# Output projection of a two-layer mixer trunk: 512 columns of w_out at a time instead of 256

## The chip, the cores and the metric

The kernel runs on one core of one Trainium2 chip. The core has five engines that run side by side: PE (TensorE: matmuls, and PEld for its weight loads), DVE (VectorE), ACT (ScalarE), POOL (GpSimd) and SP (SyncE, which here issues the DMAs). The metric is the time of one execution on the device in microseconds (us); the median of several runs counts.

## The reference, cut to what matters

Two layers run over 1024 latent tokens and 256 context tokens of 1024 channels each. At the end of a layer the three branches are merged and go through one output projection, whose result is gated and added to the stream:

```python
def _mixer_out(fa, za, u, vs, zb, attn, zc, g, w_s, b_s, w_pa, w_pb, w_pc, w_out):
    ...
    merged = ga * (ya @ w_pa) + gb * (yb @ w_pb) + gc * (yc @ w_pc)
    return merged @ w_out
...
        if not last:
            ...
            xc = xc + gate_c * out_c
        x = x + gate[:, None, :] * out
```

`w_out` is 1024 x 1024 for each layer. The context tokens are projected in layer 0 only, since nothing reads them after layer 1.

## The kernel before, in words

All of it is float32 work done as float32r: each operand is split into a rounded part and a rest (hi and lo), and `mm3` makes three matmuls of one product, hi·hi, hi·lo and lo·hi. Weights come in granules: `granule` loads 512 KB into a tile `raw` (two buffers), ACT copies it to `whi` (five buffers), DVE subtracts to get `wlo` (five buffers). A granule is thus one DMA, one ACT instruction (L212), one DVE instruction (L213).

The output projection is `out_phase`. Tokens are taken in groups: in layer 0 "C" (256 context tokens, two tiles of 128), "0" and "1" (512 latent tokens each, four tiles); in layer 1 "0" and "1". For each group it goes through `w_out` in four steps `n` of 256 columns. `w_tm` fetches a step as two granules of 512 rows x 256 columns. Within a step each tile of 128 tokens takes 24 matmuls (8 row blocks `k`, three each) into one PSUM bank, with the tokens as the stationary operand (`H[g]`, tiles named hh0C, hl1C, hh, hl, ...) and the weights as the moving one. Banks alternate between the tags `s` (three of them) and `mm` (two). Then DVE multiplies with the gate into `og` (L924) and POOL adds to the stream tile `x` (L926). When a group is done its `x` tiles are stored (L934 and L936), and in layer 0 `modulate` makes the next layer's operands of them: squares on ACT (L271), a power on POOL (L273 and L274), a scaling on DVE (L276), transposes on PE (L280) and the copies of L282 to L284.

During the first step of a group the next group's operands are made (`operands`: a load of `dM` into `ld`, L904 on ACT and L905 on DVE) and its `x` tiles are loaded (`load`, L294). SP issues all DMAs in one queue, in order, and holds at one whose buffer isn't free yet.

The order of instructions on each engine is not that of the code. A scheduler at build time moves them by its own estimates of their durations; the tiles' pools decide what has to wait for what. A pool opened where another was closed takes over its addresses, and a tile in it waits for those that lay there. `out_phase` has its small tiles in the pool `gp` (the gates `gb` 8 KB for each partition, `ld` 4 x 2 KB, `og` 4 x 1 KB). When it closes in layer 0, the next layer's `attention` opens `kp` on the same side (`kk` and `vt`, 10 KB each), and then `np`, whose first tile is `rope` (2 KB), loaded at L417 and read on POOL at L317.

Of the kernel before, what the change touches and what calls it, by code (L numbers as in the profile page):

```python
# [11 lines left out]
F32 = mybir.dt.float32  # L12
# [3 lines left out]
ALU = mybir.AluOpType  # L16
# [7 lines left out]
KC = D // 128  # L24
# [42 lines left out]
def trunk_kernel(ctx: ExitStack, tc: tile.TileContext, a: dict, out: bass.AP):  # L67
    nc = tc.nc
    PE, ACT, DVE, POOL = nc.tensor, nc.scalar, nc.vector, nc.gpsimd
# [15 lines left out]
    def bank(tag):  # L85
        tags = banks["tags"]
        tag = tag if tag in tags else "g"
        return banks["pool"].tile([128, 512], F32, tag, bufs=tags[tag])
# [118 lines left out]
    def granule(src, shape):  # L207
        raw = wp.tile(shape, F32, "raw", bufs=2)
        nc.sync.dma_start(raw, src)
        hi = wp.tile(shape, F32R, "whi", bufs=5)  # L210
        lo = wp.tile(shape, F32R, "wlo", bufs=5)
        ACT.copy(hi, raw)  # L212
        DVE.tensor_tensor(lo, raw, hi.bitcast(F32), ALU.subtract)  # L213
        return hi, lo
# [5 lines left out]
    def w_tm(w, c0):  # L220

        r = []
        for half in range(2):
            src = w[half * 512:(half + 1) * 512, c0:c0 + 256].rearrange("(k p) c -> p k c", p=128)
            r.append(granule(src, [128, 4, 256]))
        return r

    def mm3(o, lh, ll, rh, rl, start, stop):
        PE.matmul(o, lh, rh, start=start, stop=False)  # L229
        PE.matmul(o, lh, rl, start=False, stop=False)  # L230
        PE.matmul(o, ll, rh, start=False, stop=stop)  # L231
# [6 lines left out]
    def proj_tm(o, wt, h, t0):  # L238

        for k in range(KC):  # L240
            wh, wl = wt[k // 4]
            mm3(o[:, 0:256], h[0][k][:, t0:t0 + 128], h[1][k][:, t0:t0 + 128],
                wh[:, k % 4, :], wl[:, k % 4, :], k == 0, k == KC - 1)

    H = {}
# [5 lines left out]
    def new_h(g):  # L251

        n = GROUPS[g][1]
        pool = bigs["C" if g == "C" else "L"]
        halves = [[pool.tile([128, KC // 2, n], F32R, f"h{x}{i}{g}") for i in range(2)] for x in "hl"]
        H[g] = [[halves[x][k // 4][:, k % 4, :] for k in range(KC)] for x in range(2)]
        return H[g]
# [6 lines left out]
    def modulate(l, g, xts, pool):  # L264
        v = 1 if g == "C" else 0
        n = len(xts)
        hh, hl = new_h(g)
        ss = pool.tile([128, 4], F32, "ss", bufs=2)
        for i, xt in enumerate(xts):
            junk = ta().bitcast(BF16)  # L270
            ACT.activation(junk, xt, AF.Square, accum_out=ss[:, i:i + 1])  # L271
        rs = pool.tile([128, 4], F32, "rs", bufs=2)
        POOL.tensor_scalar(rs[:, :n], ss[:, :n], 1.0 / D, EPS, ALU.mult, ALU.add)  # L273
        POOL.tensor_tensor(rs[:, :n], rs[:, :n], mhalf[:, :n], ALU.pow)  # L274
        for i in range(n):
            DVE.tensor_scalar(xts[i], xts[i], rs[:, i:i + 1], None, ALU.mult)  # L276
        for k in range(KC):
            p = bank("pt")
            for i in range(n):
                PE.transpose(p[:, i * 128:(i + 1) * 128], xts[i][:, k * 128:(k + 1) * 128], ident)  # L280
            h32 = ta(n * 128)
            ACT.activation(h32, p[:, :n * 128], AF.Identity, scale=adac[l][:, 8 + k, v:v + 1], bias=adac[l][:, k, v:v + 1])  # L282
            POOL.tensor_scalar(hh[k], h32, 1.0, 0.0, ALU.mult, ALU.add)
            DVE.tensor_tensor(hl[k], h32, hh[k].bitcast(F32), ALU.subtract)  # L284

    def load_x(xp, l, t):
        xt = xp.tile([128, D], F32, "x", bufs=8)
        if t >= SEQ:
            src = a["ctx"][0, t - SEQ:t - SEQ + 128, :]
        elif l == 0:  # L290
            src = a["x"][0, t:t + 128, :]
        else:
            src = x1[t // 128]
        nc.sync.dma_start(xt, src)  # L294
        return xt
# [115 lines left out]
    def attention(l, groups, sideA, sideB, xp, wkv, X, S):  # L411
# [35 lines left out]
        def prepare(u):  # L447
            kv, g, t, pr = units[u]
            if (kv, t) not in Q:
                if kv not in W:  # L450
                    W[kv] = w_tm(a["w_in"][l], C_Q + kv * 256)
                Q[kv, t] = queries(W[kv], g, t)

        wt = wkv or w_tm(a["w_in"][l], C_KV)
        ib = 0
        names = ("C", "0", "1")
# [86 lines left out]
    def fetched(st, src, n=512, bufs=4, tag="ld"):  # L543
        t = st.tile([128, 512], F32, tag, bufs=bufs)[:, :n]
        nc.sync.dma_start(t, src)
        return t
# [7 lines left out]
    def rows(l, groups, name, col, S, st):  # L554
        w = w_tm(a["w_in"][l], col)
        for g in groups:
            g0, n = GROUPS[g]
            for i in range(n // 128):
                p = bank("mm")
                proj_tm(p, w, H[g], i * 128)  # L560
                s = staged(st, 256)
                ACT.copy(s, p[:, 0:256])
                nc.sync.dma_start(stored(S, (name, g0 // 128 + i), 256), s)
                yield 256
# [322 lines left out]
    def out_phase(l, groups, xp, gp, last, S):  # L887

        gb = gp.tile([128, 2, D], F32, "gb")
        nv = 1 if last else 2  # L890
        for v in range(nv):
            row = dp.tile([KC, 128], F32, f"gate{l}{v}")
            nc.sync.dma_start(row.rearrange("j p -> p j"), adac[l][:, 16:24, v])
            nc.sync.dma_start(gb[:, v, :], row.rearrange("j p -> (j p)").partition_broadcast(128))
        X, wt = {}, {}
        order = [g for gs in groups for g in gs]

        def operands(g):
            if g == "C":
                return  # L900
            hh, hl = new_h(g)
            for k in range(KC):
                m = fetched(gp, S["M", k, g])
                ACT.activation(hh[k], m, AF.Copy, scale=0.5)  # L904
                DVE.scalar_tensor_tensor(hl[k], m, 0.5, hh[k].bitcast(F32), ALU.mult, ALU.subtract)  # L905

        def load(g):
            g0, n = GROUPS[g]
            X[g] = [load_x(xp, l, g0 + i * 128) for i in range(n // 128)]

        wt[0] = w_tm(a["w_out"][l], 0)
        if order[0] != "C":
            operands(order[0])
        load(order[0])
        for ig, g in enumerate(order):
            gs = [g]
            for n in range(4):
                w = wt.pop(n) if n in wt else w_tm(a["w_out"][l], n * 256)
                v = 1 if g == "C" else 0
                for i, xt in enumerate(X[g]):  # L920
                    p = bank("mm" if i % 2 else "s")
                    proj_tm(p, w, H[g], i * 128)
                    t = gp.tile([128, 256], F32, "og", bufs=4)
                    DVE.tensor_tensor(t, p[:, 0:256], gb[:, v, n * 256:(n + 1) * 256], ALU.mult)  # L924
                    xs = xt[:, n * 256:(n + 1) * 256]
                    POOL.tensor_tensor(xs, xs, t, ALU.add)  # L926
                if n == 0 and ig + 1 < len(order):
                    operands(order[ig + 1])
                    load(order[ig + 1])
            for g in gs:  # L930
                g0, _ = GROUPS[g]
                for i, xt in enumerate(X[g]):
                    if last:
                        nc.sync.dma_start(out[0, g0 + i * 128:g0 + (i + 1) * 128, :], xt)  # L934
                    elif g != "C":
                        nc.sync.dma_start(x1[g0 // 128 + i], xt)  # L936
            if not last:
                for g in gs:
                    modulate(l + 1, g, X[g], xp)
# [25 lines left out]
    for l in range(DEPTH):  # L965
# [58 lines left out]
        for g in groups:  # L1024
            g0, n = GROUPS[g]
# [23 lines left out]
        xp = Pool(tc, name="xp", bufs=1, side=A)  # L1049
        gp = Pool(tc, name="gp", bufs=1, side=B)  # L1050
        out_phase(l, [["0"], ["1"]] if last else [["C"], ["0"], ["1"]], xp, gp, last, S)
        gp.close()
    xp.close()
# [62 lines left out]
```

## Time and profile before

| | |
|---|---|
| runs | 1968.52, 1967.72 and 2089.09 us, median 1968.52 |
| the profiled execution's own time | 1967.06 us |
| span of its profile | 1965.3 us |
| output projection, layer 0, group C | 985.04 to 1010.93 us of the span |
| output projection, layer 0, groups 0 and 1 | 1010.93 to 1108.40 us |
| output projection, layer 1 | 1868.09 to 1960.40 us |

The span runs from the first to the last instruction that the profiler recorded; the execution's own time has some 2 us more around it. A time such as 1010.93 is one on the span's own clock. A matmul's record starts when it is issued, and its end is modelled, so consecutive records overlap: what a matmul takes in a stream is read from the distance between two starts.

### The profile page before, as it was taken

The page shows a single profiled execution, that of the slowest core. Times are in us where ns is not written, and L with a number is a line of the kernel's source. Part 1 is how long each engine was busy: PE and PEld are TensorE (multiplying, and loading weights), DVE is VectorE, ACT ScalarE, POOL GpSimd, SP SyncE. Part 2 cuts the span into 40 slices and gives each one's busy share as a digit, 9 for nine tenths or more (in the row PEclk, how much of TensorE's full clock was granted, in tenths as well). Part 3 has the DMA queues.
Part 4 walks back from the last instruction along what each step waited for, and adds up shares of the span by engine and source line. Part 5 has one row for each costly group of instructions (what it writes and reads, how often), then busy time and mean ns, then how long its engine had stood idle before and what let it go on. Part 6 is the DMA issues. An engine that isn't in the chain of part 4 may idle for free.

```text
span 1965.3 us, 32941 instructions
## 1 busy us (share of the span) xinstructions
PE 1901.6 (97%) x11887; PEld 1688.0 (86%) x11887; DVE 1087.8 (55%) x2211; ACT 799.5 (41%) x2090; POOL 627.5 (32%) x1011
## 2 busy tenths in 40 slices
PE   7989999999999999999999989999999999999999
PEld 2888999999988887888899989899888888888898
DVE  4664665556655648766355455676665655622342
ACT  2653565445644422111243435565554443111320
POOL 1563344533331112211235543344432021211132
PEclk9999999999999999999999999999999999999999
DMA  8431121212565677654464312122134568632462
GB/s 309 119 99 64 50 68 54 79 44 84 163 188 164 188 226 227 171 174 141 148 229 165 108 47 75 54 61 82 34 91 149 158 186 270 191 106 82 134 225 87
DMA packets 281147, 259.91 MB, mean 132 GB/s; under 512 B 20824, under 2 KB 234520, under 8 KB 280984
## 3 DMA queue, kind: packets, MB, share of 16 engines
q1 hardware_dynamic: 280984, 257.80, 41.7%
q8 instruction: 94, 1.54, 0.3%
q14 instruction: 69, 0.57, 0.1%
HBM read 196.91 MB, written 60.83 MB: 131 GB/s over the span
## 4 chain that ended last, share of the span: by engine, by line
PE 82%; DMA 6%; DVE 5%; ACT 3%; issue 2%; POOL 2%; SPq 1%; POOLq 0%; DVEq 0%; ACTq 0%
PE mm L229 16%; PE mm L230 16%; PE mm L231 16%; PE s L230 6%; PE s L229 6%; PE s L231 6%; PE pt L391 3%; PE o L399 2%; PE o L398 2%; PE s L363 1%; PE s L356 1%; DVE wlo L213 1%; DMA raw<-in_w_in_dram 1%; PE s L166 1%; PE s L357 1%
## 5 line engine op out<-in xcount | busy, mean ns | idle before, releaser
L212 ACT CAST whi<-raw 128x1024 fp32r<-128x1024 f32 (+2 forms) x210 | 202.2, 966 | 393.7 <-PE s L230 144.6
L213 DVE TENSOR_TENSOR wlo<-raw,whi 128x1024 fp32r<-128x1024 f32 (+2 forms) x210 | 243.9, 1164 | 213.7 <-ACT whi L212 209.4
L229 PE MATMUL mm<-hh,whi 128*128 128x512 f32 (+1 forms) x768 | 296.2, 386 | 6.6 <-DVE st L552 4.2
L231 PE MATMUL mm<-hh,wlo 128*128 128x512 f32 (+1 forms) x768 | 294.2, 383 | 0.7 <-DVE wlo L213 0.7
L230 PE MATMUL mm<-hl,whi 128*128 128x512 f32 (+1 forms) x768 | 294.4, 383 | 0.0
L229 PE MATMUL mm<-whi,hh 128*128 128x256 f32 x832 | 239.7, 288 | 6.6 <-DVE qt L439 2.5
L231 PE MATMUL mm<-whi,hl 128*128 128x256 f32 x832 | 237.5, 285 | 0.0
L230 PE MATMUL mm<-wlo,hh 128*128 128x256 f32 x832 | 237.3, 285 | 0.0
L674 POOL TENSOR_TENSOR m<-m,tb 128x512 f32<-128x512 f32 x64 | 87.2, 1364 | 409.5 <-DVE tb L673 366.8
L229 PEld LDWEIGHTS mm<-hh,whi 128*128 128x128 f32 x768 | 145.2, 189 | 33.6 <-DVE st L552 5.1
L231 PEld LDWEIGHTS mm<-hh,wlo 128*128 128x128 f32 x768 | 145.1, 189 | 27.7 <-DVE wlo L213 0.9
L229 PEld LDWEIGHTS mm<-whi,hh 128*128 128x128 f32 x832 | 160.3, 193 | 9.0 <-issue 3.1
L230 PEld LDWEIGHTS mm<-hl,whi 128*128 128x128 f32 x768 | 145.3, 189 | 25.3
L231 PEld LDWEIGHTS mm<-whi,hl 128*128 128x128 f32 x832 | 160.5, 193 | 0.2 <-DVE hl L284 0.2
L230 PEld LDWEIGHTS mm<-wlo,hh 128*128 128x128 f32 x832 | 160.4, 193 | 0.2
L379 POOL TENSOR_SCALAR P<-P,rd 128x640 f32<-128x640 f32 (+2 forms) x144 | 110.7, 780 | 105.7 <-DVE rd L377 64.1
L230 PE MATMUL s<-hl,whi 128*128 128x512 f32 x352 | 137.5, 391 | 0.0
L229 PE MATMUL s<-hh,whi 128*128 128x512 f32 x352 | 137.4, 390 | 0.0
L231 PE MATMUL s<-hh,wlo 128*128 128x512 f32 x352 | 137.2, 390 | 0.0
L261 DVE TENSOR_TENSOR pl<-pt,ph 128x512 fp32r<-128x512 f32 (+1 forms) x184 | 112.4, 616 | 39.5 <-ACT ph L260 36.3
L260 ACT CAST ph<-pt 128x512 fp32r<-128x512 f32 (+1 forms) x184 | 96.1, 535 | 32.6 <-PE o L398 18.7
L196 DVE SCALAR_TENSOR_TENSOR aacc<-araw,scol,aacc 128x256 f32<-128x256 f32 x196 | 102.9, 558 | 5.2 <-DMA araw<-in_w_ada_dram 2.8
(303 smaller groups left out, 4637.1 us busy)
## 6 DMA issues: line engine op xcount, KB each, us to landing
raw<-in_w_in_dram SPq DMA_DIRECT2D x122, 512.0 KB, 4.1
araw<-in_w_ada_dram SPq DMA_DIRECT2D x48, 512.0 KB, 6.0
raw<-in_w_out_dram SPq DMA_DIRECT2D x40, 512.0 KB, 3.9
dP<-st SPq DMA_DIRECT2D x64, 256.0 KB, 2.7
lp<-dP SPq DMA_DIRECT2D x64, 256.0 KB, 4.2
x<-in_x_dram SPq DMA_DIRECT2D x16, 512.0 KB, 9.3
raw<-in_w_pc_dram SPq DMA_DIRECT2D x32, 256.0 KB, 2.9
dM<-m SPq DMA_DIRECT2D x32, 256.0 KB, 3.6
```

The lines of the kernel that those rows point to most:

```text
L196: DVE.scalar_tensor_tensor(acc[:, v, :], raws[k // 4][:, k % 4, :], sc, acc[:, v, :], ALU.mult, ALU.add)
L212: ACT.copy(hi, raw)
L213: DVE.tensor_tensor(lo, raw, hi.bitcast(F32), ALU.subtract)
L229: PE.matmul(o, lh, rh, start=start, stop=False)
L230: PE.matmul(o, lh, rl, start=False, stop=False)
L231: PE.matmul(o, ll, rh, start=False, stop=stop)
L260: ACT.copy(hi, src)
L261: DVE.tensor_tensor(lo, src, hi.bitcast(F32), ALU.subtract)
L379: POOL.tensor_scalar(P[hh][:, :nl + 256], P[hh][:, :nl + 256], rd[:, hh:hh + 1], 1.0, ALU.mult, ALU.mult)
L391: PE.transpose(b[:, (2 * i + hh) * 128:(2 * i + hh + 1) * 128], P[hh][:, (i0 + i) * 128:(i0 + i + 1) * 128], ident)
L398: PE.matmul(po, vs, ph[:, i * 256:(i + 1) * 256], start=(i0 + i == 0), stop=False)
L674: POOL.tensor_tensor(m, m, s, ALU.add)
```

## The change

`w_out` is now taken in two steps of 512 columns. A new function fetches a step as four granules of 256 rows x 512 columns (still 512 KB each, so 40 granules over both layers as before), every matmul of the projection has 512 moving columns in place of 256, DVE and POOL handle 512 columns at a time, and `og` has three buffers of 2 KB in place of four of 1 KB.

```diff
+    def w_half(w, n):
+
+        r = []
+        for q in range(4):
+            src = w[q * 256:(q + 1) * 256, n * 512:(n + 1) * 512].rearrange("(k p) c -> p k c", p=128)
+            r.append(granule(src, [128, 2, 512]))
+        return r
...
-        wt[0] = w_tm(a["w_out"][l], 0)
+        wt[0] = w_half(a["w_out"][l], 0)
...
-            for n in range(4):
-                w = wt.pop(n) if n in wt else w_tm(a["w_out"][l], n * 256)
+            for n in range(2):
+                w = wt.pop(n) if n in wt else w_half(a["w_out"][l], n)
                 v = 1 if g == "C" else 0
                 for i, xt in enumerate(X[g]):
                     p = bank("mm" if i % 2 else "s")
-                    proj_tm(p, w, H[g], i * 128)
-                    t = gp.tile([128, 256], F32, "og", bufs=4)
-                    DVE.tensor_tensor(t, p[:, 0:256], gb[:, v, n * 256:(n + 1) * 256], ALU.mult)
-                    xs = xt[:, n * 256:(n + 1) * 256]
+                    for k in range(KC):
+                        wh, wl = w[k // 2]
+                        c = slice(i * 128, (i + 1) * 128)
+                        mm3(p, H[g][0][k][:, c], H[g][1][k][:, c], wh[:, k % 2, :], wl[:, k % 2, :], k == 0, k == KC - 1)
+                    t = gp.tile([128, 512], F32, "og", bufs=3)
+                    DVE.tensor_tensor(t, p, gb[:, v, n * 512:(n + 1) * 512], ALU.mult)
+                    xs = xt[:, n * 512:(n + 1) * 512]
                     POOL.tensor_tensor(xs, xs, t, ALU.add)
```

The new function shifts the lines behind it by eight, so that L229 to L231 of `mm3` are L237 to L239 in the changed kernel, and so on; the text uses the numbers of the kernel before. The scheduler's order is the same up to the first output projection, and again from some way into layer 1's attention to the second one, on every engine. Three places where it differs follow.

PE, layer 1, group 0, from one step of `n` to the next. Before (the last two rows of one tile, then the next step's first tile, whose granule holds four row blocks):

```order
L230 MATMUL mm_21409<-wlo_21278,hh10_21282 128x256
L231 MATMUL mm_21409<-whi_21277,hl10_21284 128x256
L229 MATMUL s_21493<-whi_21483,hh00_21281 128x256
L230 MATMUL s_21493<-wlo_21484,hh00_21281 128x256
L231 MATMUL s_21493<-whi_21483,hl00_21283 128x256
```

And the same place with the change, from the end of the first tile's work on the second half's first granule (whi_20935 and wlo_20936 are its two parts, whi_20941 the rounded part of the second granule):

```order
L238 MATMUL s_20957<-wlo_20936,hh00_20733 128x512
L239 MATMUL s_20957<-whi_20935,hl00_20735 128x512
L237 MATMUL s_20957<-whi_20941,hh00_20733 128x512
L237 MATMUL mm_20985<-whi_20935,hh00_20733 128x512
L238 MATMUL mm_20985<-wlo_20936,hh00_20733 128x512
L239 MATMUL mm_20985<-whi_20935,hl00_20735 128x512
```

Before, a tile's 24 matmuls stand together; now the first two tiles of the second half are interleaved, granule by granule, so that the fourth granule is first needed 29 matmuls into the half and not 18.

SP, layer 0, in the middle of group C (dM_7_1 is the last stored piece of group 1's operands, `x` of in_ctx and in_x the stream tiles, raw the granules of w_out). Before:

```order
L728 DMA dM_7_1_11344<-m1_11099 128x512
L294 DMA x_11374<-in_ctx_dram 128x1024
L294 DMA x_11376<-in_ctx_dram 128x1024
L294 DMA x_11470<-in_x_dram 128x1024
L294 DMA x_11472<-in_x_dram 128x1024
L294 DMA x_11474<-in_x_dram 128x1024
L294 DMA x_11476<-in_x_dram 128x1024
L209 DMA raw_11620<-in_w_out_dram 128x4x256
L209 DMA raw_11752<-in_w_out_dram 128x4x256
L545 DMA ld_11908<-dM_7_1_11344 128x512
L294 DMA x_11912<-in_x_dram 128x1024
L294 DMA x_11914<-in_x_dram 128x1024
```

With the change (the first raw here is the last granule of group C, the second the first of group 0):

```order
L736 DMA dM_7_1_11344<-m1_11099 128x512
L302 DMA x_11386<-in_ctx_dram 128x1024
L302 DMA x_11388<-in_ctx_dram 128x1024
L302 DMA x_11482<-in_x_dram 128x1024
L302 DMA x_11484<-in_x_dram 128x1024
L302 DMA x_11486<-in_x_dram 128x1024
L302 DMA x_11488<-in_x_dram 128x1024
L553 DMA ld_11808<-dM_7_1_11344 128x512
L209 DMA raw_11508<-in_w_out_dram 128x2x512
L302 DMA x_11812<-in_x_dram 128x1024
L209 DMA raw_11640<-in_w_out_dram 128x2x512
L302 DMA x_11814<-in_x_dram 128x1024
```

Both have the same loads behind the store; the granule that group C ends on now stands behind the `ld` load as well, and the first granule of group 0 behind one more `x`.

POOL, from the last stream additions of layer 0 into layer 1 (rs and s are the norms' powers, cg the rotary tables times the gains, qf the keys of group C). Before:

```order
L926 TENSOR_TENSOR x<-x,og 128x256 x10
L273 TENSOR_SCALAR rs<-ss 128x4
L274 TENSOR_TENSOR rs<-rs,mhalf 128x4
L304 TENSOR_SCALAR s_13034<-s_13034 128x2
L305 TENSOR_TENSOR s_13034<-s_13034,mhalf 128x2
L304 TENSOR_SCALAR s_13071<-s_13071 128x2
L305 TENSOR_TENSOR s_13071<-s_13071,mhalf 128x2
L313 TENSOR_TENSOR qf<-tb,gain 128x128 x2
```

With the change:

```order
L937 TENSOR_TENSOR x<-x,og 128x512 x4
L281 TENSOR_SCALAR rs<-ss 128x4
L282 TENSOR_TENSOR rs<-rs,mhalf 128x4
L312 TENSOR_SCALAR s_12474<-s_12474 128x2
L313 TENSOR_TENSOR s_12474<-s_12474,mhalf 128x2
L312 TENSOR_SCALAR s_12511<-s_12511 128x2
L313 TENSOR_TENSOR s_12511<-s_12511,mhalf 128x2
L325 TENSOR_TENSOR cg<-rope,gain 128x64 x4
L321 TENSOR_TENSOR qf<-tb,gain 128x128 x2
```

The first four instructions on the table `rope`, which stood among the gates of layer 0 before, now stand here; and the load of `rope` on SP, which stood between the `ld` loads ahead of group C, now stands right behind the store of group 1's last `x` tile.

## Rows read from the trace of the kernel before

**Rows 1.** The page, part 1: busy time of each engine.

```profile
PE 1901.6 (97%) x11887; PEld 1688.0 (86%) x11887; DVE 1087.8 (55%) x2211; ACT 799.5 (41%) x2090; POOL 627.5 (32%) x1011
```

**Rows 2.** Windows of the output projection: length, busy times (counts), granted clock, DMA share, GB/s.

```profile
985.04:1010.93 25.89, 23.54 (x193) 23.13 (x192) 12.96 (x19) 8.24 (x11) 5.94 (x8) 1.00 0.86 294
1010.93:1108.40 97.47, 97.47 (x820) 97.47 (x819) 49.78 (x72) 38.75 (x53) 45.78 (x53) 1.00 0.45 150
1868.09:1960.40 92.31, 92.31 (x769) 92.10 (x767) 32.69 (x50) 15.56 (x17) 30.07 (x32) 1.00 0.44 155
```

**Rows 3.** Timeline of PE: start, duration, engine, line, operation.

```profile
964.63 0.40 PE L229 MATMUL mm<-hh,whi 128*128 128x512 f32 x1
...
985.04 0.28 PE L229 MATMUL s<-whi,hh0C 128*128 128x256 f32 x1
...
1002.31 0.28 PE L229 MATMUL s<-whi,hh0C 128*128 128x256 f32 x1
```

**Rows 4.** Timeline of SP in group C of layer 0: the issues.

```profile
989.59 0.32 SPq L728 DMA_DIRECT2D dM<-m  x1
...
990.91 2.60 SPq L294 DMA_DIRECT2D x<-in_x_dram  x4
993.61 1.21 SPq L209 DMA_DIRECT2D raw<-in_w_out_dram  x2
996.36 1.33 SPq L545 DMA_DIRECT2D ld<-dM  x1
```

**Rows 5.** The chain that ended last, in group C: start, length, what.

```profile
993.61 12.15 DMA raw<-in_w_out_dram
1005.84 1.05 ACT whi L212
1006.92 1.24 DVE wlo L213
1008.20 0.38 PE s L230
```

**Rows 6.** DMA issues, windows 1011 to 1108 and 1868 to 1960: KB each, median us to landing.

```profile
raw<-in_w_out_dram SPq DMA_DIRECT2D x13, 512.0 KB, 4.6
...
raw<-in_w_out_dram SPq DMA_DIRECT2D x10, 512.0 KB, 3.4
```

**Rows 7.** Timeline of ACT in layer 1's projection: in brackets the idle time before.

```profile
1889.89 1.05 ACT L212 CAST whi<-raw 128x1024 fp32r<-128x1024 f32 x1 [6.37 <-PE mm L231]
```

**Rows 8.** Timeline of DVE, POOL and SP: evictions, a 512-wide one of each, the end.

```profile
1870.33 0.68 DVE L673 SCALAR_TENSOR_TENSOR tb<-ta,pt 128x512 f32<-128x512 f32 x1
1960.51 0.42 DVE L924 TENSOR_TENSOR og<-mm,gb 128x256 f32<-128x256 f32 x1 [2.45 <-PE mm L231]
988.27 1.30 POOL L674 TENSOR_TENSOR m<-m,tb 128x512 f32<-128x512 f32 x1 [4.41 <-DVE tb L673]
1961.02 0.72 POOL L926 TENSOR_TENSOR x<-x,og 128x256 f32<-128x256 f32 x1 [2.14 <-DVE og L924]
```

**Rows 9.** Timeline of POOL, SP, DVE and PE from layer 0 into layer 1.

```profile
971.94 2.52 POOL L317 TENSOR_TENSOR cg<-rope,gain 128x64 f32<-128x64 f32 x4
...
1101.16 8.96 SPq L936 DMA_DIRECT2D x<-x  x4
...
1113.18 2.74 DVE L276 TENSOR_SCALAR x<-x,rs 128x1024 f32<-128x1024 f32 x4 [1.19 <-POOL rs L274]
...
1116.72 0.89 POOL L313 TENSOR_TENSOR qf<-tb,gain 128x128 f32<-128x128 f32 x2
...
1119.32 1.82 POOL L283 TENSOR_SCALAR hh<-ta 128x512 fp32r<-128x512 f32 x2
...
1118.14 0.38 PE L280 MATMUL pt<-ident,x 128*128 128x128 f32 x2
```

**Rows 10.** Windows right behind it, columns as in rows 2.

```profile
1131.00:1141.00 10.00, 10.00 (x86) 9.98 (x84) 7.21 (x23) 2.52 (x13) 6.74 (x17) 1.00 0.00 0
1141.00:1151.00 10.00, 6.12 (x34) 5.32 (x32) 4.85 (x10) 3.45 (x18) 5.48 (x10) 0.83 0.01 2
```

## The prediction

> **What bounds the kernel now.** I read the busy times first: PE is busy for 97% of the span, the next engine for 55% [rows 1]. An average hides stages, so I cut the output projection into windows [rows 2]. [...] Group C is different: 25.89 us, a DMA share of .86 and 294 GB/s, and PE has gaps.
>
> Then the price of a matmul, as the distance between starts [rows 3]. From 985.04 to 1002.31 stand 144 matmuls of 256 columns: 17.27 / 144 = 119.9 ns. (In layer 1, 768 in 92.31 us give 120.2.) From 964.63 to 985.04 stand 90 of 512 columns, of the stage just before: 20.41 / 90 = 226.8 ns. So 256 columns more cost 106.9 ns, and 13.1 ns of each matmul don't depend on its width. I calculate with 120.0 and 226.7: a pair of 256 takes 240 ns, one matmul of 512 takes 226.7, and a pair turned into one saves 13.3 ns.
>
> The group C gaps: 192 matmuls x 120 ns = 23.04 us of 25.89, so PE stands 2.85 us there. The chain of waits names the cause: a `w_out` granule issued at 993.61 lands 12.15 us later, then a cast of 1.05 and a subtraction of 1.24, then PE [rows 5]. That granule stands in SP's queue behind four and more 512 KB `x` loads [rows 4].
>
> **The change part by part.** 18 tiles (2 + 8 + 8) take 96 matmuls each, 1728, which become 864. If all were PE-bound, 864 x 13.3 ns = 11.5 us would go. By stage:
>
> Groups 0 and 1 of layer 0: 8 tiles x 48 = 384 matmuls x 226.7 ns = 87.04, before 768 x 120 = 92.16. The other 5.31 us of the 97.47 (transposes for the next layer) stay. Gain 5.1 us.
>
> Layer 1: the same 384 matmuls, gain 5.1 us.
>
> Group C: 96 pairs' 1.3 us is the most that could go, but the end there is set by the last granule. The first half's 48 matmuls take 10.88 us and end at 995.9, its four granules being loaded ahead. Of the second half the last granule stands behind the same `x` loads and now behind the `ld` load as well; it can land where it did (1005.76), or later by what 0.25 to 0.5 MB takes at 294 GB/s, 0.9 to 1.7 us [rows 2, 4]. I take 1006.4. Cast and subtraction make its rest ready at 1008.8 (1.05 + 1.24 and the handovers of rows 5), some ten matmuls are left by then, 2.3 us: the stage ends at 1011.1 in place of 1010.93. Cost 0.2 us, bounds -0.5 and +1.9.
>
> Group 0's start: its first granule now stands behind one more `x` load. Its rest is ready 2.3 us after it lands, while PE has come to the end of C. I take 0.5 us, from 0 to 2 (1.7 us for 0.5 MB at that rate).
>
> The borders between halves, six in all (three a layer): before, a step ran on two granules with three `whi` buffers to spare; now a half holds four of five. The half's first granule is last used 18 matmuls (4.08 us) before its end; only then can ACT cast the second granule of the next half, DVE subtract it, and SP load the fourth into its `raw`: the issue comes about 1.6 us before the border. It lands 3.4 to 4.6 us later, the medians of both stages [rows 6], so 1.8 to 3.0 us past the border, its cast (1.05) [rows 7] ends 2.9 to 4.1 past. PE wants it 29 matmuls into the half, 6.6 us past, since the first two tiles are interleaved. Cost 0; hidden up to a landing of 7.1 us. The one cover here is that interleaving: with the tiles one behind the other it would be wanted after 18 matmuls, 4.1 us past, with nothing to spare.
>
> ACT and DVE do the same bytes in half the instructions. A 512-wide DVE eviction took 0.68 us, a 256-wide one 0.42; on POOL 1.30 and 0.72 [rows 8]. Only the last of a chain is on a path. At the end of the kernel both follow PE's last matmul: 0.26 + 0.58 = 0.84 us, I take 0.9 with the output DMA of twice the columns. Cost 0.9.
>
> Entry into layer 1: the same 0.84 us stands on the last `x` tile of group 1, ahead of the norm on POOL and the scaling on DVE. In the trace DVE's four scalings end at 1115.92 and PE's transposes of them start at 1118.14 [rows 9], so about 2 us of that is covered. Two things come on top. The small pool grows from 20 to 22 KB, so `rope` now overlaps `og`: its load moves behind the store of group 1's last `x` tile (the four stores' issues end at 1110.12), and it is awaited by POOL's four `cg`, 2.52 us for four [rows 9], which now stand ahead of the `qf` (1116.72) and `hh` copies (1119.32) that PE wants. With a landing of 3.4 to 4.6 us `rope` is there at about 1114, before POOL comes to it, and the 2.52 us shift what is behind. PE has other work there: in the ten microseconds from 1131 it is busy for 10.00, in the next ten for 6.12 [rows 10]. How much of the 2.52 + 0.84 arrives at PE the trace can't say: none of it gives 0, and -0.5 if the stage above ends on less; with a late `rope` (below) up to 6. I take 1.0, nearer the covered end, because 2 of the 3.4 us are slack.
>
> The sum: -5.1 - 5.1 + 0.2 + 0.5 + 0 + 1.0 + 0.9 = -7.6 us. Span 1965.3 becomes 1957.7, the execution's own 1967.06 becomes 1959.5; the median of the runs is 1.46 us above that execution, so 1960.9, and I say 1961.0.
>
> [...] The rows say 119.9 and 226.8 ns [rows 3]. [...]
>
> **Rivals.** (1) Group C and the entry cost nothing: C then ends 0.5 earlier, the wait at group 0 and the cost at the entry are 0, which leaves -10.2 - 0.5 + 0.9 = -9.8, about 1958.7. For it: the landings are uncertain to 2 us each way. Against: C is bound by its DMAs. (2) The entry into layer 1 costs 6 us: `rope` lands as late as the granule of rows 5, 12.15 us after its issue, so at 1122.3; POOL was at 1116.72, so it waits 5.6, adds its 2.5 of `cg`, and 2 are slack. Then -7.6 + 5.0 = -2.6, 1965.9; with a dip of the clock as in the window of .83 [rows 10], up to 3 us more. Against: little else is on the queue there. (3) The slower side: the fourth granule arrives late at each of the six borders. If it landed in 12.15 us, as in group C, PE would stand 12.15 - 7.1 = 5.0 us six times, +30, giving about 1991. It decides from a landing of 7.1 us, and the kernel as a whole is slower than before from about 8.4 (six times 1.3 us eat the 7.6). Against: landings of 3.4 and 4.6 us at a DMA share of .44 and .45 [rows 2, 6]; for it: SP's one queue also carries `x`, `ld` and stores. (4) The change does not do what it says to PE: the columns are the same in number, and if a matmul of 512 with the tokens stationary takes twice 120 ns, the 10.2 us of gain are 0 and the costs stay: +2.6, about 1971. Against it: the 226.8 ns were measured in the same kernel at the same clock, with other operands. [...]
>
> **How the numbers follow.** Forecast 0.72, rival (1) 0.08, (2) 0.13, (3) 0.03, (4) 0.04. The forecast's own bounds: C -0.7 or +1.7 from its term, group 0 -0.5 or +1.5, entry -1.5 or +1; not all fall on one side, so -2.7 and +4 around 1961. The range reaches 1956.5 below, under rival (1) and with room for a run's spread, and 1967.5 above, which takes in most of rival (2); outside lie (3), (4) and the worst of (2). A measurement of this kernel can tell about 2% from no change, 39 us; even the whole 11.5 us are 0.6%. So faster by over 2% 0.01, within 0.96, slower 0.03, nearly all of it a rival (3) worse than priced.
>
> **What would show it.** In the changed kernel's trace: starts 226.7 ns apart in the projection (240: rival 4); windows of about 26 us for C, 92.4 to 93 for groups 0 and 1, 87.1 for layer 1; no wait of PE for a `whi` beyond 0.5 us at a border (rival 3: 5 us each); waits for `whi` or `wlo` in C and at the start of group 0; at the entry `rope` landed before POOL is free for `cg`, and PE's idle time up to 1151 about 1 us longer (rival 2: 6); from PE's last matmul to the end 0.9 us more. Most open are the places where the order of SP and POOL changed, C and the entry: if the sum is wrong by more than 2 us, I expect it there.

## The result and the profile after

| | before | with the change |
|---|---|---|
| median of five runs | 1967.9 us | 1957.0 us |
| profiled execution, and its span | 1967.06 us, 1965.3 us | 1954.58 us, 1952.8 us |

The ratio is 0.9949, with a 95% interval from 0.9936 to 0.9963: 7 to 13 us faster, within 2%. A second timing of the same kernel, beside other runs of the kernel before, gave 1958.13 against 1965.95 us, ratio 0.9957 (0.9944 to 0.9970), 6 to 11 us. The forecast was 1961.0, a gain of 7.6, in a range of 1956.5 to 1967.5. (The 2089.09 us among the runs before is a disturbed run and left out of every ratio.)

The page of the changed kernel, part 1 (busy time, share, instructions), answers to [rows 1]. PE has 864 instructions fewer, and 11.8 us less of modelled busy time:

```profile
PE 1889.8 (97%) x11023; PEld 1640.5 (84%) x11023; DVE 1084.8 (56%) x2175; ACT 799.5 (41%) x2090; POOL 606.6 (31%) x975
```

Its windows of the output projection (group C, groups 0 and 1, layer 1; columns as in [rows 2]):

```profile
983.68:1007.56 23.88, 22.35 (x98) 17.86 (x96) 12.26 (x15) 8.26 (x10) 4.02 (x4) 1.00 0.87 312
1007.56:1100.60 93.04, 92.96 (x434) 76.75 (x432) 49.95 (x57) 37.97 (x52) 37.29 (x37) 1.00 0.46 150
1859.88:1946.92 87.04, 87.04 (x385) 71.88 (x383) 30.27 (x34) 15.64 (x17) 21.00 (x16) 1.00 0.47 167
```

Layer 1 is what the arithmetic says, 384 x 226.7 ns, with PE busy all through. Groups 0 and 1 gave 4.3 us, counted to the first matmul of layer 1 as in the table below. Group C seems to have given 2.0, more than the 1.3 that its matmuls could give: its end is still set by the granule. The chain of waits shows that granule, this time landing after 9.47 us and not 12.15 [rows 5]:

```profile
992.52 0.66 SPq L553
993.23 9.47 DMA raw<-in_w_out_dram
1002.78 1.05 ACT whi L212
1003.86 1.24 DVE wlo L213
1005.13 0.50 PE s L238
```

PE's timeline around it (start, duration, line, tiles, in brackets the wait): PE stands for the granule's two parts. At the start of group 0 (1007.56) it stands once more for the first `wlo`: the row at 1008.01 is followed by one at 1008.48 and not at 1008.24, 0.24 us, and the next one (1008.82) comes 0.34 us behind that and not 0.23.

```profile
1003.88 0.50 PE L237 MATMUL s<-whi,hh1C 128*128 128x512 f32 x1 [1.00 <-ACT whi L212]
1004.21 0.40 PE L237 MATMUL mm<-whi,hh1C 128*128 128x512 f32 x1
1005.13 0.50 PE L238 MATMUL s<-wlo,hh1C 128*128 128x512 f32 x1 [0.53 <-DVE wlo L213]
...
1008.01 0.39 PE L237 MATMUL s<-whi,hh 128*128 128x512 f32 x1
1008.48 0.50 PE L238 MATMUL s<-wlo,hh 128*128 128x512 f32 x1
```

Because two profiled executions differ by more than a few of these terms, I read the same marks in each kernel's trace, all in us. "Ahead" is all that comes before group C. Groups 0 and 1 end at layer 1's first matmul (1108.26 before). "Entry" runs from there to the last but one pair of `qf` transposes in layer 1's attention, "between" from that mark to layer 1's projection, "end" from the end of PE's last matmul (its start plus a pitch, the distance from one start to the next in a stream) to the end of the span. No instruction changes its place in "between", and none in "ahead" but a few near its end. The kernels of the lower rows are described below.

| kernel | ahead | group C | groups 0, 1 | entry | between | layer 1 | end |
|---|---|---|---|---|---|---|---|
| before | 985.04 | 25.89 | 97.33 | 145.37 | 614.47 | 92.16 | 5.05 |
| before, again (b1) | 985.58 | 23.40 | 97.32 | 146.49 | 613.82 | 92.15 | 5.04 |
| 512 in layer 1 only (e4) | 986.71 | 23.59 | 97.32 | 146.43 | 611.95 | 87.04 | 5.86 |
| changed | 983.68 | 23.88 | 93.04 | 147.05 | 612.23 | 87.04 | 5.88 |
| changed, again (a1) | 986.26 | 23.23 | 93.00 | 147.81 | 613.11 | 87.04 | 5.84 |
| changed, two og (e3) | 985.61 | 23.60 | 93.10 | 146.28 | 613.28 | 87.04 | 5.89 |
| 256-wide, rest changed (e1) | 986.14 | 23.99 | 99.08 | 146.52 | 613.71 | 92.15 | 5.80 |
| four raw buffers (e7) | 985.71 | 21.76 | 92.68 | 148.69 | 612.62 | 87.04 | 5.80 |
| tail in two pieces (e9) | 986.71 | 24.45 | 93.02 | 147.67 | 614.95 | 87.35 | 4.05 |
| both (e11) | 985.41 | 21.76 | 92.68 | 147.08 | 615.40 | 87.35 | 4.12 |

The two columns that the change hardly touches, "ahead" and "between", scatter by 3.0 and 3.5 us from execution to execution.

### The profile page after: what moved, and what is told of

Its sections match the earlier page's. It is cut to its first block, busy times and chain, and to the rows that moved or that the text cites. A ratio compares the mean times of both kernels' runs of the same rounds, so it can differ in the third digit from the quotient of the medians.

```text
span 1952.8 us, 31098 instructions
## 1 busy us (share of the span) xinstructions
PE 1889.8 (97%) x11023; PEld 1640.5 (84%) x11023; DVE 1084.8 (56%) x2175; ACT 799.5 (41%) x2090; POOL 606.6 (31%) x975
## 4 chain that ended last, share of the span: by engine, by line
PE 81%; DMA 6%; DVE 5%; ACT 3%; issue 2%; POOL 2%; SPq 1%; POOLq 0%; DVEq 0%; ACTq 0%
PE mm L237 16%; PE mm L238 16%; PE mm L239 16%; PE s L238 6%; PE s L239 6%; PE s L237 6%; PE pt L399 3%; PE o L407 2%; PE o L406 2%; PE s L371 1%; PE s L364 1%; DMA raw<-in_w_in_dram 1%; DMA lt<-dT 1%; DVE wlo L213 1%; PE s L365 1%
## 5 line engine op out<-in xcount | busy, mean ns | idle before, releaser
L237 PE MATMUL mm<-hh,whi 128*128 128x512 f32 (+1 forms) x768 | 295.6, 385 | 6.4 <-DVE st L560 4.2
L239 PE MATMUL mm<-hh,wlo 128*128 128x512 f32 (+1 forms) x768 | 293.4, 382 | 0.7 <-DVE wlo L213 0.7
L237 PE MATMUL mm<-whi,hh 128*128 128x256 f32 (+1 forms) x704 | 217.4, 309 | 10.1 <-DVE qt L447 5.2
L238 PE MATMUL mm<-wlo,hh 128*128 128x256 f32 (+1 forms) x704 | 214.9, 305 | 0.0
L239 PE MATMUL mm<-whi,hl 128*128 128x256 f32 (+1 forms) x704 | 214.5, 305 | 0.0
L237 PEld LDWEIGHTS mm<-hh,whi 128*128 128x128 f32 x768 | 144.5, 188 | 33.6 <-DVE st L560 5.1
L239 PEld LDWEIGHTS mm<-hh,wlo 128*128 128x128 f32 x768 | 144.3, 188 | 27.8 <-DVE wlo L213 0.9
L237 PEld LDWEIGHTS mm<-whi,hh 128*128 128x128 f32 x704 | 135.5, 193 | 17.5 <-issue 5.6
L238 PEld LDWEIGHTS mm<-wlo,hh 128*128 128x128 f32 x704 | 135.5, 192 | 5.0
L239 PEld LDWEIGHTS mm<-whi,hl 128*128 128x128 f32 x704 | 135.4, 192 | 5.1 <-DVE hl L292 0.2
L237 PE MATMUL s<-hh,whi 128*128 128x512 f32 x352 | 137.4, 390 | 0.0
L239 PE MATMUL s<-hh,wlo 128*128 128x512 f32 x352 | 137.2, 390 | 0.0
```

## The experiments

All edits are to the changed kernel, if nothing else is said.

**e1, the width alone.** Granules, evictions and `og` as changed, the matmuls narrow again:

```diff
-    mm3(p, H[g][0][k][:, c], H[g][1][k][:, c], wh[:, k % 2, :], wl[:, k % 2, :], k == 0, k == KC - 1)
+    for f in range(0, 512, 256):
+        for j, (x, y) in enumerate(((0, wh), (0, wl), (1, wh))):
+            PE.matmul(p[:, f:f + 256], H[g][x][k][:, c], y[:, k % 2, f:f + 256], ...)
```

> The changed kernel (four granules a half, 512-wide evictions, three og buffers) with each 512-wide matmul of the output projection made as two of 256, column half by column half. Theory W (the gain is a fixed part of each matmul, saved once per pair): the pitch is 120 ns again, layer 1's window goes back from 87.0 to about 92.2 us, groups 0 and 1 from 93.0 to about 98, and the whole is 10 to 11 us above the changed kernel, near 1967. Rival S (the gain comes from the supply: larger rows per granule, fewer evictions): the windows stay at 87 and 93 and the time near 1957. Group C tells a second thing: it lasted 25.89 us before and 23.88 with the change; if the granules' arrival sets it, it stays near 24 with the narrow matmuls, if the matmuls' width does, it goes back to 25.9.

Measured: 1969.22 us, ratio to before 1.0016 (1.0007 to 1.0024). Its windows (group C, groups 0 and 1, layer 1):

```profile
986.14:1010.13 23.99, 23.28 (x193) 23.07 (x192) 11.28 (x14) 8.24 (x10) 4.66 (x4) 1.00 0.89 319
1010.13:1109.21 99.08, 97.83 (x818) 97.44 (x817) 53.21 (x57) 38.71 (x52) 36.04 (x37) 1.00 0.42 140
1869.45:1961.60 92.15, 92.15 (x769) 92.10 (x767) 30.36 (x34) 15.60 (x17) 20.96 (x16) 1.00 0.45 158
```

Layer 1 is back at 92.15, 768 x 120 ns, and the whole gain is gone, so it came from the width of the matmuls and not from the granules or the evictions; those by themselves cost some 3 us, by the table 1.8 in groups 0 and 1 and 0.8 at the end. Group C's 23.99 decides little: its 192 matmuls alone take 23.04, and PE is busy for 23.28.

**e8, 128 columns.** The same edit with pieces of 128.

> The changed kernel with each 512-wide matmul of the output projection as four of 128. Theory W as a straight line (13.1 ns for each matmul plus 0.4175 ns for each column): a pitch of 66.6 ns, 266 ns for 512 columns in place of 226.7, layer 1's window 102.3 us, the whole about 33 us above the changed kernel, near 1990. Rival L (the weight load of each matmul, which a shorter matmul no longer covers, sets the pitch): a pitch clearly above 66.6 ns; at 80 ns it would be 320 ns for 512 columns and layer 1's window 123 us, the whole near 2035.

Measured: 2147.19 us, ratio 1.0916 (1.0901 to 1.0930). Layer 1's window, and four rows of PE's timeline:

```profile
1967.04:2138.51 171.47, 171.47 (x1537) 171.47 (x1535) 30.95 (x34) 15.99 (x18) 20.83 (x16) 1.00 0.24 85
```

```profile
2000.04 0.28 PE L935 MATMUL mm<-whi,hl 128*128 128x128 f32 x1
2000.15 0.28 PE L935 MATMUL mm<-whi,hh 128*128 128x128 f32 x1
2000.27 0.27 PE L935 MATMUL mm<-wlo,hh 128*128 128x128 f32 x1
2000.38 0.28 PE L935 MATMUL mm<-whi,hl 128*128 128x128 f32 x1
```

171.47 us for 1536 matmuls are 111.6 ns each: rival L's kind of answer, and further off than its number. Half the columns save 8 ns. The straight line that the prediction drew through 256 and 512 ends somewhere below 256.

**e10, 320 and 192 columns.** The same edit with two unequal pieces, to tell a floor for each matmul from a limit on their average.

> The changed kernel with each 512-wide matmul of the output projection as one of 320 and one of 192. Theory M (each matmul takes the longer of its own N/2.4 + 13.3 ns and of the 111.5 ns that the 128-wide ones took, one by one): 146.6 + 111.5 = 258 ns in place of 226.7, layer 1's window 99.1 us, the whole about 26 us above the changed kernel. Rival P (what a short one lacks is covered by a long one beside it): 146.6 + 93.3 = 240 ns, window 92.2 us, 12 us above.

Measured, one execution: 1984.39 us; before, beside it, had a median of 1965.66. Layer 1's window:

```profile
1877.78:1976.76 98.98, 98.98 (x769) 98.97 (x767) 30.36 (x34) 15.62 (x17) 20.97 (x16) 1.00 0.42 147
```

98.98 / 384 = 257.8 ns for a pair. Theory M said 258, rival P 240. The edit makes three matmuls of 320 and then three of 192; over this window the mean distances to the next start are 169, 145 and 146 ns, then 88, 113 and 113. At a change of width some 24 ns move from one to the other, and the sum stays. So in this projection a matmul of N columns takes the longer of N/2.4 + 13.3 ns and about 111.5 ns, and a long neighbour doesn't cover a short one. Here 1/2.4 ns for each column is the step from 120.0 to 226.7 ns, 106.7 / 256 = 0.417; widths that alternate one by one were not run.

**e4, layer 1 alone.** The kernel before, with the changed projection where `last` is true:

```diff
+        wide = last
-            for n in range(4):
+            for n in range(2 if wide else 4):
```

> 512 columns in layer 1 only; layer 0's output projection as in the kernel before. If the stages are independent, layer 0 stays at about 25.9 us (group C) and 97.5 us (groups 0 and 1), layer 1's window is 87.0, the end after PE's last matmul 0.9 us longer than before, and the whole 4.3 us below before, near 1963.6. Rival: if the measured gain beyond the sum comes from a later stage (the entry into layer 1, the end), this kernel gains 6 us or more.

Measured: 1962.95 us, ratio 0.9977 (0.9968 to 0.9986), 3.5 us (2.8 to 6.3); the stages' sum of 4.3 lies in that interval. Its row in the table adds what I had not looked for: with the instructions of before, in the same order up to layer 1's projection, group C lasted 23.59 us and not 25.89.

**b1, the kernel before once more.**

> The kernel before, profiled once more. Its group C lasted 25.89 us in the profile shown; the kernel with 512 columns in layer 1 only has the same instructions in the same order up to layer 1's projection, and its group C lasted 23.59. Theory N (the 2.0 us by which group C was shorter with the change are a spread of the granule's landing from run to run): group C between 23.5 and 26 here, no fixed 25.9. Rival F (the four 256-row granules land faster): 25.9 again, within 0.3.

Measured: 1965.58 us. The window of its group C, and the chain of waits in it:

```profile
985.58:1008.98 23.40, 23.28 (x194) 23.07 (x192) 13.12 (x19) 8.03 (x10) 5.97 (x8) 1.00 0.93 327
```

```profile
994.29 9.53 DMA raw<-in_w_out_dram
1003.89 1.05 ACT whi L212
1004.97 1.24 DVE wlo L213
1006.25 0.38 PE s L230
```

The granule landed after 9.53 us. Theory N holds: the 12.15 of [rows 5] was one execution's landing (9.82 in e4, 9.47 and 9.04 in the two traces of the changed kernel), and the 2.0 us in group C are no work of the change. What made that one landing later is open.

**e3, two og buffers.** `bufs=3` becomes `bufs=2`; the `rope` load and the first `cg` go back to where they were before.

> The changed kernel with two og buffers of 2 KB in place of three: the small pool is 20 KB again, the rope load goes back ahead of group C and the first cg instructions back among the gates of layer 0. If the moved rope load and cg cost nothing (the trace of the changed kernel shows POOL taking 1.16 us for the four cg and PE's waits in the entry 5.8 us against 5.2 before), the time is within 0.7 us of the changed kernel's 1957. If they cost the 1.0 us of the prediction, it is faster by about that. Rival: with two buffers DVE waits for POOL and PE for banks; each tile's eviction is 0.69 + 1.26 = 1.95 us against 10.9 us of matmuls for two tiles, so a wait of PE of over 0.2 us at a tile would surprise.

Measured: 1957.01 us, ratio 0.9955 (0.9942 to 0.9967), no different from the changed kernel within the intervals. The entry takes 146.28 us, 0.8 to 1.5 less than in the two traces of the changed kernel; but e1, which has the late `rope`, took 146.52. The marks spread too much to give these tenths to `rope`. PE waits nowhere for the two `og` buffers: layer 1 stays at 87.04.

**e7, four raw buffers in the output projection.** Two granules of a half get their raw tile from the small pool:

```diff
-        raw = wp.tile(shape, F32, "raw", bufs=2)
+        raw = pool.tile(shape, F32, "rawx", bufs=2) if pool else wp.tile(shape, F32, "raw", bufs=2)
...
-            r.append(granule(src, [128, 2, 512]))
+            r.append(granule(src, [128, 2, 512], pool if q > 1 else None))
```

> The changed kernel with four raw buffers in the output projection (two of them in the small pool, two og buffers): SP's order puts all granules of group C and the first of group 0 ahead of the x loads. If only the granule behind the x loads makes PE wait there, group C falls from 23.6 to 23.9 us to its matmuls' 21.8, group 0 starts without a wait, and the whole is 2 to 2.5 us below the changed kernel, near 1954.5. Rival: the x tiles, now later, hold POOL's additions and with them the og buffers, DVE and PE's banks: PE waits in groups C or 0 and the gain is gone. At the borders of the other halves nothing should change, since the fourth granule was ready 3 us before PE wanted it.

Measured: 1953.48 us, ratio 0.9939 (0.9924 to 0.9954). Its windows of group C and of groups 0 and 1:

```profile
985.71:1007.47 21.76, 21.76 (x98) 18.02 (x97) 14.73 (x16) 10.58 (x14) 6.49 (x4) 1.00 0.95 344
1007.47:1100.15 92.68, 92.68 (x434) 76.84 (x433) 46.35 (x55) 35.78 (x49) 36.26 (x36) 1.00 0.40 139
```

Group C is now 96 x 226.7 ns and nothing else, with DMA at .95 and 344 GB/s: the same bytes, but those that PE waits for first. 0.3 us go at the start of group 0 as well.

**e9, the tail.** Layer 1's last tile, last half, in two pieces of 256 columns, each with its own eviction and store.

> The changed kernel with the last half of layer 1's last tile made as two times 256 columns, each evicted and stored by itself. If the 0.83 us longer end is the last tile's wider eviction: PE ends 0.3 us later (24 x 13.3 ns), DVE and POOL end 0.8 sooner, and the last store is 128 KB in place of 512 KB, 0.5 to 1.5 us less by the 2.7 us of the 256 KB stores; from 5.9 us after PE's last matmul to about 4, the whole 1 to 2 us below the changed kernel. Rival: the end is the fixed time of a last store, whatever its size; then only 0.5 us go.

Measured: 1957.38 us, ratio 0.9958 (0.9944 to 0.9972). In the total nothing is to be seen; in the trace the end after PE's last matmul is 4.05 us in place of 5.88 and layer 1 takes 87.35, 1.5 us less together. The last eviction on DVE and POOL:

```profile
1954.41 0.42 DVE L939 TENSOR_TENSOR og<-s,gb 128x256 f32<-128x256 f32 x1 [2.45 <-PE s L239]
...
1954.92 0.72 POOL L940 TENSOR_TENSOR x<-x,og 128x256 f32<-128x256 f32 x1 [2.14 <-DVE og L939]
```

**a1 and e11, the changed kernel again and both edits together.**

> The changed kernel, timed and profiled once more beside the kernel before. By the windows of the runs so far the change gives -4.3 us in groups 0 and 1, -5.1 in layer 1's projection, +0.8 at the end, +0.3 in group C (23.4 and 23.6 us with the instructions of before, 23.6 to 23.9 with the change) and +0.6 to +1.7 on the entry into layer 1: together -7 to -8, ratio 0.9960 to 0.9964. If something else of 3 us hides between (the first measurement said -10.9 us, 0.9949), the ratio is 0.995 or less again.

> The changed kernel with four raw buffers in the output projection and the last tile's last half in two pieces of 256 columns. By the windows of the two kernels that had one of these: group C 21.8 in place of 23.9 us, 0.4 less at the start of group 0, and an end shorter by 1.8 - 0.3 = 1.5 us; together 4 us below the changed kernel of the same call. If the two get in each other's way (the store of the last tile's first half lies among other stores), less than 3.

Measured beside the same runs of before (1965.95): 1958.13 us (0.9957, 0.9944 to 0.9970) and 1954.16 us (0.9938, 0.9923 to 0.9952). The second timing of the change is 7.8 us, so the 3 us beyond the terms didn't come again. Both edits give 4.0 us more, about what their windows say, although e7 alone had measured the same ratio; 1.5 us is less than these intervals can tell. e7 had no changed kernel timed beside it; that it beats the changed kernel rests on its windows and on e11.

## Why the prediction was right

**PE's two stages: right, and they are the gain.** Both were bound by PE before: it was busy for the whole of each window, at a granted clock of 1.00 [rows 2]. Layer 1 87.04 us (87.1 forecast), groups 0 and 1 93.0 (92.4 to 92.9 forecast with the wait). Starts stand 226.7 ns apart. Rival 4 is out; e1 shows that the width alone does it. What the 13.3 ns of each matmul are isn't shown. What failed is how far the price reaches: "13.1 ns of each matmul don't depend on its width" holds at 256, 320 and 512 and not at 192 and 128, where e10 and e8 found a floor. The sum needed only 256 and 512.

**Group C: the difference not resolved, the level wrong.** The forecast was +0.2 on 25.89. With the instructions of before the stage took 25.89, 23.40 and 23.59 us, with those of the changed kernel 23.88, 23.23 and 24.45 (e9 differs at the end only): -0.4 between the means, inside spreads of 2.5 and 1.2. The step that failed is the use of one landing of 12.15 us as a property of the stage. PE's 2.85 us of standing were that execution's too; in b1 and e4 the stage is only 0.4 and 0.6 us longer than its 23.04 us of matmuls. With the change it is 1.5 to 2.7 longer than 21.76, so the 1.3 us that the width saves there go into waiting, as forecast. In the first pair of profiles the late landing made the stage look 2.0 us better with the change, as if rival 1 had come true. Of the 4.9 us between the forecast for a profiled execution (1959.5) and 1954.58, group C is 2.2, "between" 2.2 and "ahead" 1.4, with 0.9 back in the other columns: spread of single executions, most of it where nothing was changed. The queue argument was right in kind: e7 moved the granules ahead of the `x` loads, and the wait was gone.

**Group 0's start:** 0.5 forecast, 0.35 seen in PE's rows (0.24 and 0.11), 0.3 to 0.4 by e7. A smaller term was put at nothing: the "other 5.31 us" of groups 0 and 1 don't quite stay. In e7, without that wait, 92.68 - 87.04 = 5.64 us are left for them and 97.33 - 92.16 = 5.17 in the kernel before; the distances from the 48 transposes to the next start (L280 before) add to 3.77 us before and 4.25 in the changed kernel and e7.

**The borders: right.** In layer 1 (borders at 1881.64, 1903.40 and 1925.16) ACT's casts of the changed kernel show the second granule of a half and its fourth, and what each waited for:

```profile
1877.76 1.06 ACT L212 CAST whi<-raw 128x1024 fp32r<-128x1024 f32 x1 [2.78 <-PE mm L239]
...
1883.77 1.05 ACT L212 CAST whi<-raw 128x1024 fp32r<-128x1024 f32 x1 [3.59 <-DMA raw<-in_w_out_dram]
...
1899.52 1.05 ACT L212 CAST whi<-raw 128x1024 fp32r<-128x1024 f32 x1 [12.50 <-PE mm L239]
...
1905.72 1.05 ACT L212 CAST whi<-raw 128x1024 fp32r<-128x1024 f32 x1 [3.79 <-DMA raw<-in_w_out_dram]
...
1921.28 1.05 ACT L212 CAST whi<-raw 128x1024 fp32r<-128x1024 f32 x1 [11.96 <-PE mm L239]
...
1927.13 1.05 ACT L212 CAST whi<-raw 128x1024 fp32r<-128x1024 f32 x1 [3.43 <-DMA raw<-in_w_out_dram]
```

The second granule's cast starts 3.9 us ahead of each border, when PE has left the old half's first granule; the fourth's ends 3.2, 3.4 and 3.0 us behind it (2.9 to 4.1 forecast), and PE wants it 6.6 us behind. In groups 0 and 1 no distance between PE's starts is above 0.34 us but the one at 1008.01. Rival 3 didn't come. What would happen with a later landing was not tried.

**The entry: the size right, its parts wrong.** +1.0 was forecast. The three traces with before's order gave 145.37, 146.49 and 146.43, the two of the changed kernel and e9 147.05, 147.81 and 147.67: +1.4 on the mean, with spreads of 1.1 and 0.8. `rope` was not late (issued at 1103.40, landed 4.7 us later), and the four `cg` took 1.16 us and not the 2.52 they had taken elsewhere [rows 9]:

```profile
1110.19 1.08 POOL L313 TENSOR_TENSOR s<-s,mhalf 128x2 f32<-128x2 f32 x1
1111.24 1.16 POOL L325 TENSOR_TENSOR cg<-rope,gain 128x64 f32<-128x64 f32 x4
1112.37 0.87 POOL L321 TENSOR_TENSOR qf<-tb,gain 128x128 f32<-128x128 f32 x2
```

PE's waits moved to other instructions. Before, and then with the change:

```profile
1142.30 0.41 PE L433 MATMUL mm<-ident,qf 128*128 128x128 f32 x2 [0.92 <-ACT mm L303]
1145.09 0.38 PE L356 MATMUL s<-kk,qt 128*128 128x256 f32 x1 [2.38 <-POOL qt L441]
1152.44 0.35 PE L229 MATMUL mm<-hh,whi 128*128 128x256 f32 x1 [1.90 <-DVE qt L439]
```

```profile
1131.64 0.39 PE L237 MATMUL mm<-whi,hh 128*128 128x256 f32 x1 [0.93 <-DVE vt L485]
1137.25 0.41 PE L441 MATMUL mm<-ident,qf 128*128 128x128 f32 x2 [2.18 <-DVE qf L336]
1140.31 0.55 PE L237 MATMUL mm<-whi,hh 128*128 128x256 f32 x1 [2.65 <-DVE qt L447]
1147.14 0.36 PE L237 MATMUL mm<-hh,whi 128*128 128x256 f32 x1 [1.37 <-DVE qt L447]
```

These add to 5.2 us before and 7.1 with the change. Which of the moved instructions makes the 1.4 us is open. e3 took `rope` and `cg` back, and PE still waits at the same four places there, for 0.62, 2.19, 2.39 and 1.37 us: 6.6 in all, so they are at most a small part of it.

**The end:** 0.9 forecast, 0.8 measured (5.04 to 5.86). It is the last tile's wider eviction alone. These two rows of the changed kernel are 0.27 and 0.54 us longer than those of before [rows 8]:

```profile
1947.19 0.69 DVE L935 TENSOR_TENSOR og<-mm,gb 128x512 f32<-128x512 f32 x1 [4.75 <-PE mm L239]
1947.96 1.26 POOL L937 TENSOR_TENSOR x<-x,og 128x512 f32<-128x512 f32 x1 [4.15 <-DVE og L935]
```

From POOL's end to the end of the span it is 3.5 us in both kernels. In e9 that stretch is 2.6: of its 1.8 us, 0.8 are the eviction and 0.9 the last store, 128 KB in place of 512.

By the table's means, over the three traces with the order of before and the three with the changed one where each applies, the terms add to -4.3 - 5.1 - 0.4 + 1.4 + 0.8 = -7.6 us, the forecast to the tenth. That exactness is luck, since group C and the entry scatter by 1 us and more; the two PE terms and the end are not. The timings said 10.9, 7.8 and, for e3, 9.4, each with an interval of 5 us or so that holds 7.6.

## What to carry to other kernels

Read a matmul's price from the distance between starts at two widths in the same trace before widening it; here a matmul cost 13.3 ns beside its columns at 256 and more, and about 111.5 ns at 192 and 128. The two lines meet at an estimated 236 columns, (111.5 - 13.3) x 2.4. A single landing time read from one execution is not a level: profile the kernel before twice before pricing a wait of a few microseconds by it. And where PE waits for one transfer among many, as in group C here, look at the order of the queue before the width: two more raw buffers brought the stage to its bare matmuls (21.76 us in e7), some 2 us that the wider matmuls alone didn't give.

## What the runs showed of the hardware that I had not expected

A floor under a matmul with a weight load of its own: 111.6 ns at 128 columns (e8), and 257.8 ns for 320 and 192 columns together (e10), which is 146.6 + 111.2. At 256 columns the pitch of 120 ns is 8 ns above that floor, so the old kernel was close to the point where narrower matmuls stop being cheaper. PE's weight loads in e8 start at the same pitch, 0.11 and 0.12 us apart:

```profile
2000.09 0.19 PEld L935 LDWEIGHTS mm<-whi,hh 128*128 128x128 f32 x1
2000.20 0.19 PEld L935 LDWEIGHTS mm<-wlo,hh 128*128 128x128 f32 x1
2000.32 0.19 PEld L935 LDWEIGHTS mm<-whi,hl 128*128 128x128 f32 x1
```

The kernel before has the floor in its own trace, at one column. Of its eight matmuls of L200, each with a weight load of its own, seven stand 111 or 112 ns ahead of PE's next start (the first stands 26 ns ahead). And two bfloat16 matmuls of 128 columns with their own loads (L354) take 0.10 us together. The granted clock is 1.00 at both places. So not every pair of load and matmul has this floor:

```profile
839.22 0.95 PE L200 MATMUL o<-ones,aacc 128*128 128x1 f32 x8
...
1403.82 0.29 PE L354 MATMUL s<-maskb,identb 128*128 128x128 bf16 x2
1403.92 0.42 PE L356 MATMUL s<-kk,qt 128*128 128x384 f32 x1
```

The recorded weight loads differ as well: 187 to 192 ns for each of the eight float32 ones at L200, 96 and 99 ns for the two bfloat16 ones at L354. So both places fit a floor that comes with the float32 weight load. That the load itself sets it is my guess and not shown, since no kernel here ran such matmuls without one.

The landing of one 512 KB granule behind the same loads took 9.53, 9.82 and 12.15 us in three executions of the same instructions. POOL's four `cg` took 2.52 us among the gates of layer 0 (the kernel before, and e3) and 1.16 at the entry into layer 1 (the changed kernel); why is open.
